# The causal convolution of a float32 block: VectorE's taps added in place in the PSUM bank, fewer taps on TensorE and GpSimd, weight splits of the stage on GpSimd

## The chip, the core and the metric

One core of one Trainium2 chip runs the whole program in one launch. The metric is device time in microseconds (us); lower is better. The kernel before took 2717.13 us (median of three runs, 2713.91 to 2719.76).

## What is computed

A block with a residual stream x of 512 tokens by 1024 features, in float32: two attention layers, four feed-forward modules, a state-space module and a convolution module. The change lies in the convolution module alone:

```python
def conv_mixer(h, w_in, b_in, dw, dw_b, ln_g, ln_b, w_out, b_out):
    z = h @ w_in + b_in
    a, g = jnp.split(z, 2, axis=-1)
    z = a * jax.nn.sigmoid(g)
    z = lax.conv_general_dilated(z, dw[:, None, :].astype(z.dtype), window_strides=(1,),
                                 padding=[(CONV_W - 1, 0)],
                                 dimension_numbers=('NWC', 'WIO', 'NWC'),
                                 feature_group_count=D_MODEL) + dw_b
    z = jax.nn.silu(layernorm(z, ln_g, ln_b))
    return z @ w_out + b_out
```

CONV_W is 31 and each of the 1024 features has its own 31 weights: y[t] is the sum over 31 taps of dw[tap] * z[t - 30 + tap]. One tap over a tile of 128 features by 512 tokens is a multiplication by one number per feature and an addition.

## The kernel before

Features stand on the 128 partitions, so the 1024 features of the convolution are eight tiles, f0 to f7, of 128 x 512. Matrices are multiplied at float32 accuracy in three passes of float32r matmuls (`mm3`, lines 159 to 161): every operand is kept as a high part and a low part, and high x high, high x low and low x high are added up in PSUM. Weights are streamed from DRAM by `load` (line 134): a DMA on SP's queue, a copy to the high part on ScalarE (line 148), and the low part as the difference on VectorE, or on GpSimd for the tile numbers in `self.on_pool` and for the first four tiles of a stage (line 153). In this stage `on_pool` is empty. A tile is 128 x 1024, and a feature tile of the input projection takes two.

`conv` (line 1165) is a software pipeline over the eight feature tiles, with three steps.

- `enter(f)`: the input projection (48 matmuls of 512 columns; f0 and f1 go together, in halves of 256 columns), the sigmoid on ScalarE (line 1208), z = a * sigmoid on VectorE (line 1211, out of PSUM, into a tile of 542 columns with 30 zeros ahead). Then the accumulator b: its first tap on ScalarE (line 1214), and further taps in which ScalarE makes the product (line 1184) and GpSimd adds it (line 1185). Then z is split in two parts for TensorE (lines 1218, 1219).
- `taps(f)`, one turn later: the first NTAP[f] taps on TensorE. GpSimd writes diagonal matrices of the weights (line 1230), and three matmuls of 512 columns for each tap add up in a PSUM bank `pc` (two banks take turns, `pjav`). The taps that are left go to VectorE, each one SCALAR_TENSOR_TENSOR in place on b (line 1187).
- `leave(f)`, three turns after `enter`: y = b + pc in another order of tokens (VectorE, line 1242), and a matmul with ones that gathers the mean (line 1244).

The 31 taps of a tile are shared out by two tables, which give 76 taps to TensorE, 52 to ScalarE with GpSimd (8 of them ScalarE's first ones, so 44 additions on line 1185), and 120 to VectorE:

```python
CLAG = 1, 3
NTAP, PTAP = (6, 6, 7, 8, 10, 10, 14, 15), (6, 8, 8, 8, 8, 8, 4, 2)
```

Behind the loop come the variance (lines 1256 to 1267), the normalisation with SiLU (lines 1272, 1273) and the output projection. A scheduler sets each engine's order of instructions when the program is built, so work of neighbouring feature tiles is interleaved on every engine, and engines then run their queue in order, held by semaphores.

Of the kernel before, what the change touches and what calls it, by code (L numbers as in the profile page):

```python
# [14 lines left out]
P = 128  # L15
# [50 lines left out]
class Kern:  # L66
# [30 lines left out]
    # how many tiles of a kind are alive at most; kinds of one size share a count  # L97
# [83 lines left out]
    def pow_(self, r, n):  # L181
        """r ^ -0.5 in place"""
        self.nc.gpsimd.tensor_tensor(out=r, in0=r, in1=self.mh.to_broadcast([P, n]), op=ALU.pow)  # L183

    def rsq(self, ss, n, div, eps):
        """(ss / div + eps)^-0.5"""
        r = self.st(n)
        self.nc.gpsimd.tensor_scalar(out=r, in0=ss, scalar1=1.0 / div, scalar2=eps, op0=ALU.mult, op1=ALU.add)
        self.pow_(r, n)
        return r  # L190

# [1 line left out]
    def prenorm(self, xt, g, dest, t):  # L193
        """xt [128, 1024] natural; dest(k0) -> AP [128, 4, 2, 128] for k0 = 0, 4"""
# [14 lines left out]
    def to_parts(self, src, dst):  # L209
        """src [128, 512] natural -> dst [128, 4, 2, 128]: transposed, split"""  # L210
        nc = self.nc
        tp = self.ps("tp", [P, 4, P])
        for i in range(4):
            nc.tensor.transpose(tp[:, i], src[:, i * P:(i + 1) * P], self.ident)  # L214
        self.splith(dst[:, :, 0], dst[:, :, 1], tp)
# [6 lines left out]
    def chain(self, t, y0, ss0, ps1, gpost, mul, nxt, bias=None):  # L222
        """x_t += rms(y_t) * gpost * mul (y0 is already times gpost), then the next norm"""
# [18 lines left out]
    def half0(self, ps, gpost, mul, bias=None):  # L242
        """the first half of y: sum of squares and y * gpost in SBUF"""
# [17 lines left out]
    def out_proj(self, key0, key1, lhs, gpost, mul, nxt, bias=None, group=1):  # L261
        """y = lhs @ w (8 k tiles), natural, then chain; lhs(k, t) -> (h, l);
        in the first half of y the token tiles go together by groups"""
# [87 lines left out]
    def attn(self, l, nxt):  # L351
# [3 lines left out]
        # tables and small parameters of the layer  # L355
# [27 lines left out]
        def roped(ab, rq):  # L383
            # ab [128, 2 (cos, sin), groups, 2, 16] -> rq [128, groups, 2, 16]
# [20 lines left out]
        def chunk_d(ci):  # L405
# [6 lines left out]
            for t in range(T):  # L412
# [15 lines left out]
                # q: [h h l l], k: [h l h l]  # L428
# [95 lines left out]
        # gates: silu(g) = g * (1 + tanh(g / 2)) / 2, the half is in the heads' factors  # L524
# [117 lines left out]
        def unit_out(u):  # L642
            """[vh|vl]^T P^T summed over the parts and turned, then the head's norm"""
# [29 lines left out]
            # (sum + 64 eps d1^2)^-0.5; the factor 8 is in sub  # L673
# [36 lines left out]
        # projections emitted along with the units  # L710
# [15 lines left out]
        def advance(f, end):  # L726
            """a projection goes on to its next step"""
# [93 lines left out]
    def sincos(self, cos, sin, y, n):  # L821
# [23 lines left out]
        # quadrant  # L845
# [43 lines left out]
    def s5_params(self):  # L889
# [23 lines left out]
        # discretised input matrix factor  # L913
# [18 lines left out]
        # |a|^4 and the unit phasor of a^4 with its doublings  # L932
# [9 lines left out]
        # cos and sin of phi * chunk for the first 16 chunks, by doubling  # L942
# [7 lines left out]
    def double(self, dst, src, s, js, m):  # L950
        """chunks m to 2m of dst from chunks 0 to m of src"""
# [9 lines left out]
    def s5_batch(self, b):  # L961
        """the matrices of four pairs of groups, in steps"""
# [9 lines left out]
        def cprod(src, w, re, im, negative):  # L972
            """(re, im) = src * w, or its conjugate"""
# [10 lines left out]
        # the place of the input matrices is free now  # L984
# [10 lines left out]
        # state output  # L995
# [9 lines left out]
        # Toeplitz part  # L1005
# [20 lines left out]
    def s5(self, nxt):  # L1026
# [20 lines left out]
        def enter(n):  # L1047
            """the chunks of four pairs, turned, times the input matrices"""
# [29 lines left out]
        def rotate_back(n):  # L1078
# [6 lines left out]
            # the state before each chunk  # L1085
# [57 lines left out]
        # the first four together: the last features come late  # L1143
# [16 lines left out]
    HOOK = 3, 1.5  # L1160
    CLAG = 1, 3
    GRP = 2, 2
    NTAP, PTAP = (6, 6, 7, 8, 10, 10, 14, 15), (6, 8, 8, 8, 8, 8, 4, 2)

    def conv(self, nxt):
# [14 lines left out]
        def tap(out, z, f, i, pool=False):  # L1180
            w = cp[:, f, 5 + i:6 + i]
            if pool:
                prod = self.tl("tap", [P, 512])
                nc.scalar.activation(prod, z[:, i:i + 512], AF.Copy, scale=w)  # L1184
                g.tensor_tensor(out=out, in0=out, in1=prod, op=ALU.add)  # L1185
            else:
                v.scalar_tensor_tensor(out=out, in0=z[:, i:i + 512], scalar=w, in1=out, op0=ALU.mult, op1=ALU.add)  # L1187

        def project(fs):
            """the first two halves of the features go together, by halves of the tokens"""  # L1190
# [11 lines left out]
        def enter(f):  # L1202
            npe, ndv = self.NTAP[f], self.NTAP[f] + self.PTAP[f]
# [9 lines left out]
            b = self.tl("cb", [P, 512])  # L1213
            nc.scalar.activation(b, z[:, npe:npe + 512], AF.Identity, scale=cp[:, f, 5 + npe:6 + npe], bias=cp[:, f, 2:3])
            for i in range(npe + 1, ndv):
                tap(b, z, f, i, True)
            zz = self.tl("zz", [P, 2, 542], F32R)
            nc.scalar.activation(zz[:, 0], z, AF.Copy)
            g.tensor_tensor(out=zz[:, 1], in0=z, in1=zz[:, 0].bitcast(F32), op=ALU.subtract)
            F[f].update(z=z, zz=zz, b=b)  # L1220

        def taps(f):
            npe, ndv = self.NTAP[f], self.NTAP[f] + self.PTAP[f]
            z, zz, b = F[f]["z"], F[f]["zz"], F[f]["b"]
# [9 lines left out]
            for i in range(ndv, 31):  # L1234
                tap(b, z, f, i)

        def leave(f):
            """from the order of time to the order of the token tiles"""
# [6 lines left out]

        for i in range(8 + self.CLAG[1]):
            for stage, lag in ((enter, 0), (taps, self.CLAG[0]), (leave, self.CLAG[1])):
                if 0 <= i - lag < 8:
                    stage(i - lag)
        ident2 = self.ident.unsqueeze(1).to_broadcast([P, 2, P])  # L1250
        t2 = "p (t c) -> p t c"
        for hf in range(2):
# [7 lines left out]
            # the variance stands on every partition: its diagonal blocks give a column per token  # L1260
# [81 lines left out]
def _layout(np, a):  # L1342
    """the inputs, laid out for the loads"""
# [25 lines left out]
    # feature order of the state-space part: (j, g2, h), group g = j + 32 g2  # L1369
# [49 lines left out]
    def bd(v):  # L1419
        # v [64 groups, 64 states, 16] -> [(g2, p), 32, (g2, h)], zero off the diagonal blocks  # L1420
# [39 lines left out]
```

## Time and profile before

| | |
|---|---|
| median of three runs | 2717.13 us (2713.91 to 2719.76) |
| profiled execution: span from its first to its last instruction | 2716.2 us |
| TensorE busy in it | 2579.7 us (95%) |
| VectorE busy | 1522.4 us (56%) |
| ScalarE busy | 1043.4 us (38%) |
| GpSimd busy | 709.4 us (26%) |
| HBM traffic | 239.61 MB read, 20.97 MB written |

The profile gives no time of its own for the profiled execution beside its span; the span lies 0.9 us below the median of the runs and inside their range. The shares are averages over stages with different limits, so the stage of the change has to be read by itself. In the rows, PE is TensorE's matmuls, PEld its weight loads, DVE VectorE, ACT ScalarE, POOL GpSimd; `L1187` is line 1187 of the program above, and `t` stands for any tile. A row's duration and the distance from one start to the next are different things, and both are used.

### The profile page before, as it was taken

The page shows a single profiled execution, that of the slowest core. Times are in us where ns is not written, and L with a number is a line of the kernel's source. Part 1 is how long each engine was busy: PE and PEld are TensorE (multiplying, and loading weights), DVE is VectorE, ACT ScalarE, POOL GpSimd, SP SyncE. Part 2 cuts the span into 40 slices and gives each one's busy share as a digit, 9 for nine tenths or more (in the row PEclk, how much of TensorE's full clock was granted, in tenths as well). Part 3 has the DMA queues.
Part 4 walks back from the last instruction along what each step waited for, and adds up shares of the span by engine and source line. Part 5 has one row for each costly group of instructions (what it writes and reads, how often), then busy time and mean ns, then how long its engine had stood idle before and what let it go on. Part 6 is the DMA issues. An engine that isn't in the chain of part 4 may idle for free.

```text
span 2716.2 us, 34572 instructions
## 1 busy us (share of the span) xinstructions
PE 2579.7 (95%) x13512; PEld 2190.4 (81%) x13512; DVE 1522.4 (56%) x2301; ACT 1043.4 (38%) x1977; POOL 709.4 (26%) x892
## 2 busy tenths in 40 slices
PE   8998999989999999899999999999999768999998
PEld 7987899878888888888888888888888546888887
DVE  7787587885688722694533324333226997533322
ACT  5567554675334422323422223322225323422221
POOL 4652245522265500331200002000006872200000
PEclk9999999999999999899999999999999889999999
DMA  4221232112235523442222222222222001222221
GB/s 148 74 66 62 78 108 74 61 62 83 82 136 198 196 98 127 149 177 94 97 97 94 94 101 86 101 95 96 97 101 86 31 31 41 99 93 96 98 94 70
DMA packets 68899, 262.81 MB, mean 97 GB/s; under 512 B 7936, under 2 KB 8448, under 8 KB 64384
## 3 DMA queue, kind: packets, MB, share of 16 engines
q1 hardware_dynamic: 68736, 260.61, 27.4%
q8 instruction: 106, 1.74, 0.3%
q14 instruction: 57, 0.47, 0.1%
HBM read 239.61 MB, written 20.97 MB: 96 GB/s over the span
## 4 chain that ended last, share of the span: by engine, by line
PE 47%; DVE 6%; POOL 2%; issue 1%; ACT 0%; POOLq 0%; DVEq 0%; ACTq 0%
PE t L160 15%; PE t L161 15%; PE t L159 15%; DVE t L1187 4%; POOL t L1230 1%; DVE t L153 1%; POOL t L153 0%; POOL t L1185 0%; PE t L214 0%; DVE t L1242 0%; DVE t L1256 0%; DVE t L1211 0%; ACT t L200 0%; PE t L1102 0%; ACT t L232 0%
## 5 line engine op out<-in xcount | busy, mean ns | idle before, releaser
L159 PE MATMUL t<-t,t 128*128 128x512 f32 (+2 forms) x3596 | 1320.8, 369 | 39.3 <-DVE t L1242 21.8
L160 PE MATMUL t<-t,t 128*128 128x512 f32 (+2 forms) x3596 | 1321.2, 368 | 8.8 <-DVE t L167 3.6
L161 PE MATMUL t<-t,t 128*128 128x512 f32 (+2 forms) x3596 | 1318.5, 368 | 2.5 <-DVE t L167 2.4
L153 DVE TENSOR_TENSOR t<-t,t 128x1024 fp32r<-128x1024 f32 (+2 forms) x326 | 413.3, 1270 | 723.5 <-ACT t L148 488.1
L159 PEld LDWEIGHTS t<-t,t 128*128 128x128 f32 x3596 | 681.6, 190 | 159.4 <-issue 17.1
L160 PEld LDWEIGHTS t<-t,t 128*128 128x128 f32 x3596 | 683.3, 190 | 124.8 <-DVE t L167 6.4
L161 PEld LDWEIGHTS t<-t,t 128*128 128x128 f32 x3596 | 682.6, 190 | 117.2 <-DVE t L167 4.2
L148 ACT ACTIVATE t<-t 128x1024 fp32r<-128x1024 f32 (+2 forms) x370 | 384.2, 1045 | 535.1 <-PE t L160 454.7
L235 POOL TENSOR_SCALAR t<-t,t 128x1 f32<-128x1 f32 x32 | 10.7, 334 | 1327.2 <-ACT t L232 1325.9
L166 ACT ACTIVATE t<-t 128x512 fp32r<-128x512 f32 (+3 forms) x316 | 155.6, 517 | 298.0 <-DVE t L297 121.2
L167 DVE TENSOR_TENSOR t<-t,t 128x512 fp32r<-128x512 f32 (+3 forms) x316 | 199.1, 647 | 81.9 <-ACT t L166 81.7
L153 POOL TENSOR_TENSOR t<-t,t 128x512 fp32r<-128x512 f32 (+4 forms) x90 | 162.2, 1820 | 66.2 <-ACT t L148 52.4
L296 ACT ACTIVATE t<-t 128x512 f32<-128x512 f32 x88 | 52.6, 598 | 301.5 <-PE t L161 295.7
L1187 DVE SCALAR_TENSOR_TENSOR t<-t,t,t 128x512 f32<-128x512 f32 x120 | 143.4, 1240 | 3.7 <-POOL t L1185 2.7
L555 ACT ACTIVATE t<-t,t 128x512 f32<-128x512 f32 (+1 forms) x176 | 113.5, 654 | 39.6 <-DVE t L553 37.2
L553 DVE TENSOR_REDUCE t<-t 128x1 f32<-128x512 f32 (+1 forms) x160 | 105.6, 681 | 16.2 <-PE t L571 7.5
L297 DVE TENSOR_TENSOR t<-t,t 128x512 f32<-128x512 f32 x88 | 60.5, 687 | 83.0 <-PE t L161 82.7
L621 DVE TENSOR_TENSOR t<-t,t 128x512 fp32r<-128x512 f32 x112 | 76.1, 685 | 36.1 <-ACT t L616 29.7
L1185 POOL TENSOR_TENSOR t<-t,t 128x512 f32<-128x512 f32 x44 | 78.5, 1786 | 25.3 <-ACT t L1184 23.2
L958 POOL TENSOR_TENSOR t<-t,t 128x64 f32<-128x64 f32 (+3 forms) x112 | 65.8, 606 | 66.3 <-DVE t L886 48.3
L183 POOL TENSOR_TENSOR t<-t,t 128x1 f32<-128x1 f32 (+2 forms) x98 | 74.0, 756 | 6.9
L976 DVE TENSOR_TENSOR t<-t,t 128x256 f32<-128x256 f32 x128 | 65.3, 574 | 17.7 <-DMA t<-in_s5bc 17.4
(220 smaller groups left out, 2228.8 us busy)
## 6 DMA issues: line engine op xcount, KB each, us to landing
t<-in_W SPq DMA_DIRECT2D x356, 512.0 KB, 3.5
mats<-t SPq DMA_DIRECT2D x16, 1024.0 KB, 4.3
t<-mats SPq DMA_DIRECT2D x16, 1024.0 KB, 6.1
t<-in_gv SPq DMA_DIRECT2D x19, 512.0 KB, 4.1
t<-in_W SPq DMA_DIRECT2D x24, 384.0 KB, 3.2
t<-in_W SPq DMA_DIRECT2D x8, 480.0 KB, 4.1
t<-in_x SPq DMA_DIRECT2D x4, 512.0 KB, 7.1
t<-in_mem SPq DMA_DIRECT2D x4, 512.0 KB, 6.3
```

What stands on the lines that cost most here:

```text
L148: nc.scalar.activation(h[:, :c], raw[:, :c], AF.Copy)
L153: eng.tensor_tensor(out=l[:, o:o + m], in0=raw[:, o:o + m], in1=h[:, o:o + m].bitcast(F32), op=ALU.subtract)
L159: mm(out, lhs[0], rhs[0], start=start, stop=False)
L160: mm(out, lhs[0], rhs[1], start=False, stop=False)
L161: mm(out, lhs[1], rhs[0], start=False, stop=stop)
L166: nc.scalar.activation(h, src, AF.Copy)
L167: nc.vector.tensor_tensor(out=l, in0=src, in1=h.bitcast(F32), op=ALU.subtract)
L553: v.tensor_reduce(out=mx[:, q * w:q * w + w], in_=part, axis=AX.X, op=ALU.max, negate=True)
L555: act.activation(e[:, i], part[:, i - q * w], AF.Exp, bias=mx[:, i:i + 1], accum_out=u["d"][:, i:i + 1])
L621: v.tensor_tensor(out=lo, in0=tp, in1=h.bitcast(F32), op=ALU.subtract)
L1185: g.tensor_tensor(out=out, in0=out, in1=prod, op=ALU.add)
L1187: v.scalar_tensor_tensor(out=out, in0=z[:, i:i + 512], scalar=w, in1=out, op0=ALU.mult, op1=ALU.add)
```

## The change

The diff, without lines that only lose a comment:

```diff
-    CLAG = 1, 3
+    CLAG = 1, 1, 2
+    CPOOL = tuple(range(12))
     GRP = 2, 2
-    NTAP, PTAP = (6, 6, 7, 8, 10, 10, 14, 15), (6, 8, 8, 8, 8, 8, 4, 2)
+    NTAP, PTAP = (6, 6, 6, 6, 6, 6, 7, 8), (4, 5, 5, 5, 5, 5, 4, 3)
...
         def enter(f):
...
-            b = self.tl("cb", [P, 512])
-            nc.scalar.activation(b, z[:, npe:npe + 512], AF.Identity, scale=cp[:, f, 5 + npe:6 + npe], bias=cp[:, f, 2:3])
-            for i in range(npe + 1, ndv):
-                tap(b, z, f, i, True)
             zz = self.tl("zz", [P, 2, 542], F32R)
             nc.scalar.activation(zz[:, 0], z, AF.Copy)
             g.tensor_tensor(out=zz[:, 1], in0=z, in1=zz[:, 0].bitcast(F32), op=ALU.subtract)
+            b = self.tl("cb", [P, 512])
+            nc.scalar.activation(b, z[:, npe:npe + 512], AF.Identity, scale=cp[:, f, 5 + npe:6 + npe], bias=cp[:, f, 2:3])
+            for i in range(npe + 1, npe + npl):
+                prod = self.tl("tap", [P, 512])
+                nc.scalar.activation(prod, z[:, i:i + 512], AF.Copy, scale=cp[:, f, 5 + i:6 + i])
+                g.tensor_tensor(out=b, in0=b, in1=prod, op=ALU.add)
...
         def taps(f):
...
-            for i in range(ndv, 31):
-                tap(b, z, f, i)
+
+        def more(f):
+
+            z, pc = F[f]["z"], F[f]["pc"]
+            for i in range(self.NTAP[f] + self.PTAP[f], 31):
+                v.scalar_tensor_tensor(out=pc, in0=z[:, i:i + 512], scalar=cp[:, f, 5 + i:6 + i], in1=pc, op0=ALU.mult, op1=ALU.add)
...
-        for i in range(8 + self.CLAG[1]):
-            for stage, lag in ((enter, 0), (taps, self.CLAG[0]), (leave, self.CLAG[1])):
+        self.on_pool = self.CPOOL
+        for i in range(8 + self.CLAG[2]):
+            for stage, lag in ((enter, 0), (taps, self.CLAG[0]), (more, self.CLAG[1]), (leave, self.CLAG[2])):
                 if 0 <= i - lag < 8:
                     stage(i - lag)
+        self.on_pool = ()
```

By the new tables TensorE has 51 taps (25 fewer, 75 matmuls fewer), ScalarE and GpSimd 36 (28 additions on GpSimd instead of 44), and VectorE 161 instead of 120. VectorE's taps no longer add onto the SBUF tile b but onto the PSUM bank in which TensorE has just added up its own; they come behind the matmuls of their tile. All twelve weight tiles of f2 to f7 have their low part made on GpSimd instead of VectorE (the four of f0 and f1 were there already, in halves). `leave` comes two turns after `enter` instead of three. The z tile is split for TensorE ahead of GpSimd's taps.

Three places in the built programs. The first is VectorE's queue where the z of a late feature tile is made. In the kernel before, at f6 (L1187 is a tap, its first name the tile it adds onto; L1211 z; L1242 `leave`):

```order
L1211 SCALAR_TENSOR_TENSOR t3205_19016<-t3202_18964,t2_64,t3204_19014 128x4x128 [waits Activation_49]
L1187 SCALAR_TENSOR_TENSOR t3162_18735<-t3161_18732,t2_64,t3162_18735 128x512 [waits DVE_49]
L1187 SCALAR_TENSOR_TENSOR t3140_18598<-t3139_18595,t2_64,t3140_18598 128x512 [waits DVE_49]
L1187 SCALAR_TENSOR_TENSOR t3183_18873<-t3182_18870,t2_64,t3183_18873 128x512 [waits Pool_49]
L1187 SCALAR_TENSOR_TENSOR t3162_18735<-t3161_18732,t2_64,t3162_18735 128x512 [waits DVE_49]
L1242 TENSOR_TENSOR t3195_18949<-t3140_18598,t3171_18761 128x512 [waits DVE_49]
L1187 SCALAR_TENSOR_TENSOR t3183_18873<-t3182_18870,t2_64,t3183_18873 128x512 [waits DVE_49]
L1187 SCALAR_TENSOR_TENSOR t3162_18735<-t3161_18732,t2_64,t3162_18735 128x512 [waits DVE_49]
L1187 SCALAR_TENSOR_TENSOR t3183_18873<-t3182_18870,t2_64,t3183_18873 128x512 [waits DVE_49]
L1187 SCALAR_TENSOR_TENSOR t3162_18735<-t3161_18732,t2_64,t3162_18735 128x512 [waits DVE_49]
```

and in the changed one, at f7 (L1235 is a tap, L1204 z):

```order
L1235 SCALAR_TENSOR_TENSOR t3176_18856<-t3150_18707,t2_64,t3176_18856 128x512 [waits DVE_49]
L1235 SCALAR_TENSOR_TENSOR t3193_18981<-t3169_18836,t2_64,t3193_18981 128x512 [waits DVE_49]
L1242 TENSOR_TENSOR t3195_19023<-t3152_18713,t3176_18856 128x512 [waits DVE_49]
L1204 SCALAR_TENSOR_TENSOR t3205_19090<-t3202_19038,t2_64,t3204_19088 128x4x128 [waits Activation_49]
L1235 SCALAR_TENSOR_TENSOR t3193_18981<-t3169_18836,t2_64,t3193_18981 128x512 [waits DVE_49] x11
L1235 SCALAR_TENSOR_TENSOR t3210_19104<-t3187_18964,t2_64,t3210_19104 128x512 [waits PE_49,Pool_49]
L1235 SCALAR_TENSOR_TENSOR t3193_18981<-t3169_18836,t2_64,t3193_18981 128x512 [waits DVE_49]
L1235 SCALAR_TENSOR_TENSOR t3210_19104<-t3187_18964,t2_64,t3210_19104 128x512 [waits DVE_49]
L1235 SCALAR_TENSOR_TENSOR t3193_18981<-t3169_18836,t2_64,t3193_18981 128x512 [waits DVE_49]
```

Before, taps of two or three feature tiles alternate, each on an SBUF tile. Now they are on PSUM banks (t3176, t3193 and t3210 are the banks of f4, f5 and f6), the first tap of a bank waits for TensorE, and between stretches that alternate stand runs on one bank, such as the eleven of f5. In the whole queue the tap in front is on the same bank for 90 of the 161 taps; before, it was on the same tile for 28 of 120.

The second place is GpSimd's queue at the start of the loop. Before (L1185 is an addition of a product, L1219 the low part of z, L1230 diagonal matrices):

```order
L1185 TENSOR_TENSOR t3089_18307<-t3089_18307,t3090_18309 128x512 [waits Activation_49]
L1185 TENSOR_TENSOR t3089_18307<-t3089_18307,t3091_18312 128x512 [waits Activation_49,Pool_49]
L1185 TENSOR_TENSOR t3089_18307<-t3089_18307,t3092_18315 128x512 [waits Activation_49,Pool_49]
L1219 TENSOR_TENSOR t3095_18324<-t3088_18304,t3095_18324 128x542 [waits DVE_49,Activation_49]
L1185 TENSOR_TENSOR t3089_18307<-t3089_18307,t3093_18318 128x512 [waits Pool_49]
L1230 TENSOR_TENSOR t3108_18359<-t2_64,t1_63 128x768
L1230 TENSOR_TENSOR t3108_18359<-t2_64 128x768
L1185 TENSOR_TENSOR t3089_18307<-t3089_18307,t3094_18321 128x512 [waits Pool_49]
L1185 TENSOR_TENSOR t3098_18332<-t3098_18332,t3099_18334 128x512 [waits Activation_49]
L1219 TENSOR_TENSOR t3106_18355<-t3097_18329,t3106_18355 128x542 [waits DVE_49,Activation_49]
L1185 TENSOR_TENSOR t3098_18332<-t3098_18332,t3100_18337 128x512 [waits Pool_49]
L1185 TENSOR_TENSOR t3098_18332<-t3098_18332,t3101_18340 128x512 [waits Activation_49,Pool_49]
```

and in the changed program (L1214, L1208 and L1226 are the same three things, L153 a weight split):

```order
L153 TENSOR_TENSOR t3106_18389<-t3104_18386,t3105_18388 128x1024 [waits DMAHW0_49,PE_49,Activation_49]
L153 TENSOR_TENSOR t3109_18395<-t3107_18392,t3108_18394 128x1024 [waits DMAHW2_49,PE_49,Activation_49]
L1208 TENSOR_TENSOR t3089_18307<-t3088_18304,t3089_18307 128x542 [waits Activation_49]
L1214 TENSOR_TENSOR t3090_18310<-t3090_18310,t3091_18312 128x512 [waits Activation_49]
L1214 TENSOR_TENSOR t3090_18310<-t3090_18310,t3092_18315 128x512 [waits Activation_49,Pool_49]
L153 TENSOR_TENSOR t3125_18518<-t3123_18515,t3124_18517 128x1024 [waits DMAHW3_49,PE_49,Activation_49]
L1214 TENSOR_TENSOR t3090_18310<-t3090_18310,t3093_18318 128x512 [waits Pool_49]
L1226 TENSOR_TENSOR t3103_18344<-t2_64,t1_63 128x768
L1226 TENSOR_TENSOR t3103_18344<-t2_64 128x768
L153 TENSOR_TENSOR t3128_18524<-t3126_18521,t3127_18523 128x1024 [waits DMAHW4_49,PE_49,Activation_49]
L1208 TENSOR_TENSOR t3096_18326<-t3095_18323,t3096_18326 128x542 [waits Activation_49]
L1214 TENSOR_TENSOR t3097_18329<-t3097_18329,t3098_18331 128x512 [waits Activation_49]
```

The low part of f0's z is now ahead of the additions, and four weight splits of 128 x 1024 have come in between (eight more follow).

The third place is TensorE's queue near the end of the loop in the changed program, where the matmul with ones for f4 (L1244) stands ahead of the taps of f6, which go into the same bank as f4's:

```order
L159 MATMUL t3193_18981<-t3170_18839,t3194_18982 128x512
L160 MATMUL t3193_18981<-t3170_18839,t3194_18982 128x512
L161 MATMUL t3193_18981<-t3170_18839,t3194_18982 128x512
L1244 MATMUL t3070_18077<-t3195_19023,t2_64 128x512 [waits DVE_49]
L159 MATMUL t3210_19104<-t3188_18967,t3211_19105 128x512 [waits Activation_49,Pool_49]
L160 MATMUL t3210_19104<-t3188_18967,t3211_19105 128x512
L161 MATMUL t3210_19104<-t3188_18967,t3211_19105 128x512 [waits Pool_49]
L159 MATMUL t3210_19104<-t3188_18967,t3211_19105 128x512
```

Both wait until VectorE has finished all of f4's taps and its `leave`; TensorE runs its queue in order.

## Rows read from the trace of the kernel before

**Rows 1.** The page: busy tenths of the span in 40 slices of 67.9 us.

```profile
PE   8998999989999999899999999999999768999998
DVE  7787587885688722694533324333226997533322
```

**Rows 2.** Stretches: us, PE, PEld, DVE, ACT, POOL busy (instructions), PE clock, DMA share, GB/s.

```profile
2079.00:2277.00 198.00, 144.20 (x572) 110.38 (x570) 182.48 (x155) 56.42 (x83) 144.25 (x80) 0.87 0.13 46
2125.00:2141.00 16.00, 1.30 (x4) 0.53 (x3) 16.00 (x16) 2.68 (x5) 7.63 (x7) 0.63 0.19 66
1900.00:1980.00 80.00, 80.00 (x348) 65.13 (x347) 21.02 (x20) 18.21 (x20) 0.00 (x0) 1.00 0.29 99
```

**Rows 3.** Chain of waits, 2050 to 2300 us: shares by line; start, us, what.

```profile
by line: DVE t L1187 44.6%; issue 7.0%; PE t L160 6.8%; PE t L161 6.6%; PE t L159 6.6%; POOL t L1230 5.9%; DVE t L153 5.3%; POOL t L1185 3.6%; DVE t L1242 2.8%; DVE t L1256 2.2%; DVE t L1211 2.1%; POOL t L1219 1.4%; DVE t L1272 1.1%; PE t L
...
2095.66 1.79 DVE t L1187
...
2273.72 1.06 DVE t L1242
2274.83 1.14 PE t L1244 x2
```

**Rows 4.** Groups, 2079 to 2277 us: count | busy us, mean ns | idle before, releasers.

```profile
L1187 DVE SCALAR_TENSOR_TENSOR t<-t,t,t 128x512 f32<-128x512 f32 x120 | 143.4, 1240 | 3.7 <-POOL t L1185 2.7
L1185 POOL TENSOR_TENSOR t<-t,t 128x512 f32<-128x512 f32 x44 | 78.5, 1786 | 25.3 <-ACT t L1184 23.2
L153 DVE TENSOR_TENSOR t<-t,t 128x1024 fp32r<-128x1024 f32 x15 | 25.8, 1723 | 10.6 <-ACT t L148 9.1 <-PE t L160 1.5
L1211 DVE SCALAR_TENSOR_TENSOR t<-t,t,t 128x512 f32<-128x512 f32 x8 | 9.0, 1130 | 0.0
L1242 DVE TENSOR_TENSOR t<-t,t 128x512 f32<-128x512 f32 x8 | 8.5, 1062 | 1.6 <-PE t L161 1.6
```

**Rows 5.** VectorE in order of time: start us, us from first start to last end.

```profile
2262.16 10.20 DVE L1187 SCALAR_TENSOR_TENSOR t<-t,t,t 128x512 f32<-128x512 f32 x13
...
2186.10 6.04 DVE L1187 SCALAR_TENSOR_TENSOR t<-t,t,t 128x512 f32<-128x512 f32 x9
...
2166.07 11.94 DVE L1187 SCALAR_TENSOR_TENSOR t<-t,t,t 128x512 f32<-128x512 f32 x7
...
2161.41 1.12 DVE L1211 SCALAR_TENSOR_TENSOR t<-t,t,t 128x512 f32<-128x512 f32 x1
2162.38 1.41 DVE L1187 SCALAR_TENSOR_TENSOR t<-t,t,t 128x512 f32<-128x512 f32 x1
```

**Rows 6.** GpSimd in order of time, the same columns.

```profile
2090.48 1.47 POOL L1230 TENSOR_TENSOR t<-t,t 128x768 fp32r<-128x768 f32 x1
...
2160.90 2.34 POOL L1230 TENSOR_TENSOR t<-t 128x1024 fp32r<-128x1024 f32 x1
...
2167.32 10.14 POOL L1185 TENSOR_TENSOR t<-t,t 128x512 f32<-128x512 f32 x6
...
2259.04 1.26 POOL L1185 TENSOR_TENSOR t<-t,t 128x512 f32<-128x512 f32 x1
2260.26 1.32 POOL L1219 TENSOR_TENSOR t<-t,t 128x542 fp32r<-128x542 f32 x1
```

**Rows 7.** Groups of the whole span, shapes apart: weight splits on GpSimd.

```profile
L153 POOL TENSOR_TENSOR t<-t,t 128x1024 fp32r<-128x1024 f32 x18 | 44.9, 2502 | 10.4 <-ACT t L148 9.2 <-PE t L161 1.1
```

**Rows 8.** Groups, 1700 to 2055 us (last: 1930 to 2330): L167 reads PSUM, L153 not.

```profile
L153 DVE TENSOR_TENSOR t<-t,t 128x1024 fp32r<-128x1024 f32 x62 | 75.9, 1224 | 199.7 <-ACT t L148 130.5 <-issue 65.8 <-PE t L160 3.3
L167 DVE TENSOR_TENSOR t<-t,t 128x512 fp32r<-128x512 f32 x24 | 16.3, 684 | 0.0
...
L167 DVE TENSOR_TENSOR t<-t,t 128x256 fp32r<-128x256 f32 x16 | 6.1, 420 | 1.6 <-ACT t L166 1.6
```

**Rows 9.** VectorE, then ScalarE, in order of time (L1256 reads PSUM and SBUF).

```profile
2275.99 5.39 DVE L1256 SCALAR_TENSOR_TENSOR t<-t,t 128x256 f32<-128x256 f32 x16 [1.22 <-PE t L1244]
...
2078.08 0.69 ACT L1208 ACTIVATE t<-t,t 128x512 f32<-128x512 f32 x1 [0.39 <-PE t L161]
```

More of the change, by code (lines that the diff above doesn't have):

```diff
@@ L1178, in conv @@
         cs = []
[L1180 to L1187, printed above, removed]
         def project(fs):
@@ L1202, in enter @@
         def enter(f):
-            npe, ndv = self.NTAP[f], self.NTAP[f] + self.PTAP[f]
+            npe, npl = self.NTAP[f], self.PTAP[f]
             if f != 1:
@@ L1219, in enter @@
             g.tensor_tensor(out=zz[:, 1], in0=z, in1=zz[:, 0].bitcast(F32), op=ALU.subtract)
+            b = self.tl("cb", [P, 512])
[4 more added lines that the diff above has]
+                g.tensor_tensor(out=b, in0=b, in1=prod, op=ALU.add)
             F[f].update(z=z, zz=zz, b=b)
         def taps(f):
-            npe, ndv = self.NTAP[f], self.NTAP[f] + self.PTAP[f]
-            z, zz, b = F[f]["z"], F[f]["zz"], F[f]["b"]
+            npe = self.NTAP[f]
+            zz = F[f]["zz"]
             F[f]["pc"] = pc = self.pjav()
```

## The prediction

> **What bounds the kernel now.** The page comes first. Over the whole span TensorE is the busy engine, but in its slices [rows 1] there is one dip, slices 32 to 35, in which PE falls to 6 and 7 tenths while DVE stands at 9. That is the convolution, so the page's average is of no use here. The stretches come next [rows 2]: from the first z to the last mean (2079 to 2277 us, 198 us) VectorE is busy 182.5 us, GpSimd 144.3 and TensorE 144.2, and for 16 us from 2125 TensorE does next to nothing. In the chain of waits [rows 3] VectorE's taps, line 1187, hold 44.6% of 2050 to 2300 us, and the last link ahead of the variance is `leave` at 2273.72 and the matmul for the mean, which ends at 2275.97. So this stage ends when VectorE has done its taps, and a change is worth here what it takes off VectorE's queue.
>
> The groups tell what those taps cost [rows 4]: 120 take 143.4 us, 1.24 us each. The rows in order of time [rows 5] show three prices. Nine that alternate between tiles, with GpSimd held up all the while, take 6.04 us, 0.67 each. Thirteen on one tile, with GpSimd at rest, take 10.20 us, 0.785 each: a tap that waits for the tap just ahead of it pays 0.115 us more. And seven that run against GpSimd take 11.94 us, 1.71 each, while the six GpSimd additions of that stretch take 10.14, 1.69 each, where one alone takes 1.26 [rows 6]: addition and tap run one for one, and a pair of them needs 1.7 us. Both have two inputs in SBUF. Line 1211, which reads one input from PSUM, starts at 2161.41 in the middle of a GpSimd instruction of 2.34 us and still takes 1.12 us, its usual duration [rows 4 to 6]. An instruction with one input in PSUM does not take part in this.
>
> **What the change does to VectorE.** The 120 taps and their 143.4 us go, and so do ten of the twelve weight splits, 10 x 1.72 = 17 us [rows 4] (the other two lie ahead of 2079). There come 161 taps whose inputs are one of SBUF and one of PSUM. By the row of line 1211 they are free of GpSimd. No instruction before writes to PSUM from VectorE, so the price of one has to be bounded. From below: line 1256 reads PSUM and takes 5.39 / 16 = 0.34 us for 256 elements [rows 9], and 256 elements more cost 0.684 - 0.420 = 0.26 (line 167 in two sizes, [rows 8]), hence 0.60, or 0.715 behind its own predecessor. From above: line 1211, also out of PSUM and with a scalar per feature, lets the next instruction start 0.97 us after itself [rows 5], 0.30 more than an SBUF tap, but its strided order is a likely cause. I take the SBUF prices, 0.67 and 0.785, because they are for the same instruction with the same scalar, and because reading PSUM shows no surcharge: at 0.264 us per 256 elements line 167 takes 0.16 us over the streaming of its 512 elements out of PSUM, and line 153 takes 1.224 us for 1024 out of SBUF, 0.17 over it [rows 8]. By the orders above, 90 of the 161 follow a tap on their own bank: 90 x 0.785 + 71 x 0.67 = 118.2 us.
>
> [...]
>
> **When the first tap can start.** It now waits for TensorE's taps of f0. In TensorE's new order these stand behind the rest of f1's projection (46 matmuls of 256 columns), all 48 of f2 and nine of f3. From 2078.1 us, when TensorE has released f0's sigmoid [rows 9], that is 46 x 0.115 + (48 + 9 + 18) x 0.23 = 22.5 us, at 80 us / 348 = 0.23 us for 512 columns [rows 2] and half of it for 256; the end of the last matmul adds some 0.4. So the first tap starts near 2101, against 2095.66 before, and VectorE mostly rests until then. GpSimd is not later: behind f0's z it has the low part, two additions, a split of 2.50, an addition and two diagonal matrices of 1.47 [rows 6, 7], about 11 us from 2081.
>
> **The sum.** From 2101: taps 118.2; five z at 0.97 = 4.9; eight `leave` at 1.0 (the 1.06 of [rows 4] less the overlap with the next) = 8; four splits for the output projection, which stay on VectorE and still have two SBUF inputs, at 1.72 = 6.9; waits for TensorE at the change of banks, some five of 1 us = 5. Together 143 us, to 2244; the mean behind the last `leave` adds 1.2 [rows 3], 2245.2. Before it was 2276.0. The stage loses 30.8 us, and what follows is unchanged. The profiled execution's span of 2716.2 becomes 2685.4; it lies 0.9 us below the median of the runs shown (2717.13), so I forecast 2686.3, rounded **2686 us**.
>
> **What the other edits cost.** TensorE loses 75 matmuls of 0.23, 17 us, worth nothing by itself: from 2101 it has 366 matmuls of 0.23 and eight means of some 1.2 us left, 94 us beside VectorE's 143, which hides them. If VectorE's time fell under 94, TensorE would be next. GpSimd's part from 2079 on is ten splits of 2.50, sixteen rows of diagonal matrices (27 us), eight low parts of 1.32 and 28 additions of 1.26 [rows 6, 7], 98 us without VectorE in its way; the 165 us from first z to last mean cover it too. The splits now stand in GpSimd's queue among additions that wait for ScalarE, so a late product would delay the next weights; ScalarE loses 16 products and has room, busy 56 of 198 us [rows 2]. Splitting z first and `leave` a turn earlier cost nothing beside VectorE's queue, and SP's DMAs are the same in number and order.
>
> **Rivals.** (1) **TensorE's taps come too late** for VectorE near the end. The taps of f6 go into f4's bank and stand behind f4's mean, so TensorE rests until `leave`; then VectorE has about ten taps on the other bank, 7.9 us, in which TensorE must do the mean (1.14) and 18 matmuls (4.1). At full clock the 5.2 us fit. After pauses the granted clock fell before: 0.63 on the mean over the 16 us of rest [rows 2]. [...] Against it: the pauses are shorter, about 8 us. (2) **The tap in PSUM is dear**, the one that ends on the other side: reading and writing one bank in the same instruction, which no row shows, could cost as line 1211 does, 0.30 us more on each of 161, 48 us: 2734, slower. It decides from 30.8 / 161 = 0.19 us a tap on. A mild surcharge, up to 0.10 us a tap, is counted within the forecast. For it speaks only that nothing here was measured; against it the PSUM reads without surcharge [rows 8]. (3) **The contention stays**, because one SBUF input is enough for it: some fifty GpSimd instructions from 2101 on would each cost VectorE 1.7 - 0.7 = 1.0 us: 2736. Line 1211's undisturbed 1.12 us speaks against it. (4) The gain is given back in the following stages, or the taps do not move: the built order shows all 161 on banks, and nothing behind the mean changes, so I give this little.
>
> **How the numbers follow.** Forecast 0.73, rival 1 0.12, rival 2 0.09, rival 3 0.04, no difference 0.02. The forecast's own range: at the lower price (71 x 0.60 + 90 x 0.715 = 107), without waits (5) and with splits at 1.22 each [rows 8] (2) 18 us less, 2668; with a third of line 1211's surcharge, 0.10 us a tap, 16 more, 2702. For 8 in 10 the range runs from 2671 to 2707: it takes in rival 1 and leaves out most of rivals 2 and 3. About 0.2%, 5.4 us, is what a measurement of this kernel can tell from no change. Faster by more than that: 0.85, from the forecast and rival 1; within it 0.02; slower 0.13, from rivals 2 and 3.
>
> **What would show it.** In the profile after, 161 taps on line 1235, 0.67 or 0.785 us from one to the next, the same beside GpSimd as without it; GpSimd's additions near 1.26 instead of 1.79; the first tap near 22 us behind the first z and the last mean 165 us behind it (before 196.8); VectorE with almost no pauses in between. Taps 0.95 us apart mean rival 2; one that is long only beside GpSimd, rival 3; VectorE idle ahead of the first tap of a bank, with TensorE named, rival 1. The forecast is wrong if the stage shortens as said and the whole does not.

## The result, and the profile after

The changed kernel takes 2684.53 us (median of four runs, 2680.91 to 2690.54), beside 2717.61 us for the kernel before on the same chip (four runs, 2713.91 to 2719.76). The ratio is 0.9884, with a 95% interval of 0.9868 to 0.9899: some 32 us faster. 2686 us were forecast, in a range of 2671 to 2707. The profiled execution took 2685.91 us, with a span of 2684.1.

In the stage's slices of the page, PE stays under 9 tenths in two (33 and 34), where in [rows 1] it did in three (32 to 34; the prediction's "32 to 35" is one too many). The other digits under 9 lie outside the stage:

```profile
PE   7998999989999999989999999999999966999998
DVE  7788577875589832595533323433324697533322
```

The first z starts at 2076.58 us and the last mean ends at 2242.2, so the stage takes 165.6 us where it took 196.8; what follows it takes 441.9 (before 440.2). The stretches, with the columns of [rows 2]; the first is the stage from first z to last mean:

```profile
2076.00:2243.00 167.00, 124.20 (x502) 94.68 (x500) 137.13 (x184) 47.16 (x68) 97.96 (x68) 0.86 0.16 57
...
2099.00:2151.00 52.00, 52.00 (x222) 41.47 (x221) 47.40 (x64) 17.12 (x24) 46.94 (x35) 1.00 0.21 72
2151.00:2203.00 52.00, 36.05 (x131) 26.42 (x129) 49.78 (x67) 14.99 (x21) 28.43 (x21) 0.84 0.11 41
2203.00:2243.00 40.00, 13.16 (x30) 7.18 (x30) 36.25 (x52) 0.34 (x2) 0.00 (x0) 0.61 0.07 26
```

VectorE is busy 137.1 of 167 us, and from its first tap on it hardly rests: 133.4 of 144 us in the last three rows. GpSimd fell from 144.3 us to 98.0. Which prices did this is in the groups of the stage, first VectorE's, then GpSimd's; they answer to [rows 4]:

```profile
L1235 DVE SCALAR_TENSOR_TENSOR t<-t,t,t 128x512 f32<-128x512 f32 x161 | 116.3, 752 | 10.9 <-PE t L161 7.5
L1204 DVE SCALAR_TENSOR_TENSOR t<-t,t,t 128x512 f32<-128x512 f32 x8 | 9.1, 1142 | 21.0 <-ACT t L1201 21.0
L1242 DVE TENSOR_TENSOR t<-t,t 128x512 f32<-128x512 f32 x8 | 8.4, 1053 | 0.1
L153 DVE TENSOR_TENSOR t<-t,t 128x1024 fp32r<-128x1024 f32 x4 | 4.9, 1222 | 1.1 <-ACT t L148 1.1
...
L1214 POOL TENSOR_TENSOR t<-t,t 128x512 f32<-128x512 f32 x28 | 37.5, 1339 | 2.0 <-ACT t L1213 1.1
L153 POOL TENSOR_TENSOR t<-t,t 128x1024 fp32r<-128x1024 f32 x11 | 26.4, 2409 | 4.9 <-ACT t L148 4.6 <-issue 0.3
```

There are 161 taps in place of 120, and they take 116.3 us in place of 143.4: 0.752 us each against 1.240. A GpSimd addition takes 1.34 us against 1.79. VectorE in order of time, with the columns of [rows 5], shows that GpSimd no longer counts for a tap:

```profile
2098.76 13.42 DVE L1235 SCALAR_TENSOR_TENSOR t<-t,t,t 128x512 f32<-128x512 f32 x17 [3.67 <-PE t L161]
2113.40 6.02 DVE L1235 SCALAR_TENSOR_TENSOR t<-t,t,t 128x512 f32<-128x512 f32 x9 [1.22 <-PE t L161]
...
2121.29 11.83 DVE L1235 SCALAR_TENSOR_TENSOR t<-t,t,t 128x512 f32<-128x512 f32 x15
...
2187.06 7.34 DVE L1235 SCALAR_TENSOR_TENSOR t<-t,t,t 128x512 f32<-128x512 f32 x11 [0.32 <-PE t L161]
...
2219.63 7.34 DVE L1235 SCALAR_TENSOR_TENSOR t<-t,t,t 128x512 f32<-128x512 f32 x11 [0.59 <-PE t L161]
...
2227.84 11.04 DVE L1235 SCALAR_TENSOR_TENSOR t<-t,t,t 128x512 f32<-128x512 f32 x14
```

And GpSimd beside the fifteen taps from 2121.29 on:

```profile
2121.32 2.41 POOL L153 TENSOR_TENSOR t<-t,t 128x1024 fp32r<-128x1024 f32 x1 [4.59 <-ACT t L148]
2123.70 1.47 POOL L1226 TENSOR_TENSOR t<-t,t 128x768 fp32r<-128x768 f32 x1
2125.13 1.47 POOL L1226 TENSOR_TENSOR t<-t 128x768 fp32r<-128x768 f32 x1
2126.55 1.37 POOL L1208 TENSOR_TENSOR t<-t,t 128x542 fp32r<-128x542 f32 x1
2127.88 1.30 POOL L1214 TENSOR_TENSOR t<-t,t 128x512 f32<-128x512 f32 x1
2129.13 2.42 POOL L153 TENSOR_TENSOR t<-t,t 128x1024 fp32r<-128x1024 f32 x1
2131.50 4.05 POOL L1214 TENSOR_TENSOR t<-t,t 128x512 f32<-128x512 f32 x3
```

GpSimd works without a pause here, and the fifteen taps on one bank take 11.83 us, 0.79 each. The fourteen from 2227.84, with GpSimd at rest, take 11.04, 0.79 each too. Nine that alternate between banks take 6.02, 0.67 each. These are the two prices of [rows 5] for a tap on an SBUF tile without GpSimd in its way, to within 0.01 us. In the whole trace a tap follows a tap 148 times: 90 times by 0.77 to 0.80 us, 54 times by 0.65 to 0.67, and the four longer distances are the waits for TensorE. So no tap is slowed by GpSimd.

### The profile page after: what moved, and what is told of

Read it like the earlier page. It is cut to its first block, busy times and chain, and to the rows that moved or that the text cites. A ratio compares the mean times of both kernels' runs of the same rounds, so it can differ in the third digit from the quotient of the medians.

```text
span 2684.1 us, 34384 instructions
## 1 busy us (share of the span) xinstructions
PE 2558.3 (95%) x13437; PEld 2170.8 (81%) x13437; DVE 1471.3 (55%) x2330; ACT 1034.2 (39%) x1961; POOL 666.4 (25%) x880
## 4 chain that ended last, share of the span: by engine, by line
PE 51%; DVE 3%; POOL 1%; ACT 1%; issue 0%; DVEq 0%; POOLq 0%; ACTq 0%
PE t L160 17%; PE t L161 17%; PE t L159 17%; DVE t L1235 2%; POOL t L153 0%; PE t L1244 0%; PE t L214 0%; PE t L1261 0%; DVE t L1242 0%; ACT t L200 0%; ACT t L148 0%; ACT t L232 0%; PE t L1102 0%; DVE t L206 0%; PE t L1103 0%
## 5 line engine op out<-in xcount | busy, mean ns | idle before, releaser
L159 PE MATMUL t<-t,t 128*128 128x512 f32 (+3 forms) x3571 | 1309.5, 369 | 15.2 <-ACT t L166 12.3
L160 PE MATMUL t<-t,t 128*128 128x512 f32 (+3 forms) x3571 | 1308.8, 367 | 6.8 <-DVE t L167 3.3
L161 PE MATMUL t<-t,t 128*128 128x512 f32 (+3 forms) x3571 | 1304.5, 367 | 2.5 <-DVE t L167 2.4
L159 PEld LDWEIGHTS t<-t,t 128*128 128x128 f32 x3571 | 674.4, 189 | 133.8 <-ACT t L166 17.4
L153 DVE TENSOR_TENSOR t<-t,t 128x1024 fp32r<-128x1024 f32 (+2 forms) x314 | 389.8, 1244 | 706.1 <-ACT t L148 510.8
L160 PEld LDWEIGHTS t<-t,t 128*128 128x128 f32 x3571 | 675.7, 189 | 123.1 <-DVE t L167 6.0
L161 PEld LDWEIGHTS t<-t,t 128*128 128x128 f32 x3571 | 675.4, 189 | 115.1 <-DVE t L167 4.2
L167 DVE TENSOR_TENSOR t<-t,t 128x512 fp32r<-128x512 f32 (+3 forms) x316 | 198.9, 647 | 75.4 <-ACT t L166 75.2
L153 POOL TENSOR_TENSOR t<-t,t 128x512 fp32r<-128x512 f32 (+4 forms) x102 | 191.0, 1889 | 78.8 <-ACT t L148 56.8
L1235 DVE SCALAR_TENSOR_TENSOR t<-t,t,t 128x512 f32<-128x512 f32 x161 | 116.3, 752 | 10.9 <-PE t L161 7.5
L206 DVE SCALAR_TENSOR_TENSOR t<-t,t,t 128x512 f32<-128x512 f32 x72 | 57.9, 845 | 26.9 <-POOL t L183 26.9
```

Source lines behind the costliest of these rows:

```text
L153: eng.tensor_tensor(out=l[:, o:o + m], in0=raw[:, o:o + m], in1=h[:, o:o + m].bitcast(F32), op=ALU.subtract)
L159: mm(out, lhs[0], rhs[0], start=start, stop=False)
L160: mm(out, lhs[0], rhs[1], start=False, stop=False)
L161: mm(out, lhs[1], rhs[0], start=False, stop=stop)
L1235: v.scalar_tensor_tensor(out=pc, in0=z[:, i:i + 512], scalar=cp[:, f, 5 + i:6 + i], in1=pc, op0=ALU.mult, op1=ALU.add)
```

## The experiments

Each edit is against the changed kernel. "The loop" is the time from the start of the first z to the end of the last mean. All medians are of runs beside the kernel before on the same chip, 2719.27 us for the first four and 2716.10 for the last four.

| kernel | median, us | ratio to before (95%) | loop, us |
|---|---|---|---|
| taps back on the SBUF tile | 2733.56 | 1.0053 (1.0038 to 1.0068) | 208.3 |
| splits back on VectorE | 2691.91 | 0.9898 (0.9884 to 0.9913) | 168.1 |
| tables of before | 2688.63 | 0.9886 (0.9869 to 0.9902) | 166.9 |
| taps in PSUM alone | 2675.37 | 0.9839 (0.9825 to 0.9854) | 151.9 |
| the change again | 2687.28 | 0.9893 (0.9876 to 0.9911) | 165.6 |
| taps in PSUM alone, again | 2677.31 | 0.9858 (0.9841 to 0.9874) | 151.7 |
| tables between | 2672.82 | 0.9841 (0.9826 to 0.9856) | 147.5 |
| leave a step later | 2671.28 | 0.9836 (0.9820 to 0.9851) | 151.6 |

### Taps back on the SBUF tile

```diff
         def more(f):
-            z, pc = F[f]["z"], F[f]["pc"]
+            z, b = F[f]["z"], F[f]["b"]
...
-                v.scalar_tensor_tensor(out=pc, ... in1=pc, op0=ALU.mult, op1=ALU.add)
+                v.scalar_tensor_tensor(out=b, ... in1=b, op0=ALU.mult, op1=ALU.add)
```

> The changed kernel with one thing undone: VectorE's 161 taps add onto the SBUF tile b again; tables, splits on GpSimd and lags stay. Theory (the gain is the place of the taps: one input in PSUM keeps them out of GpSimd's way): 161 taps at 0.72 us, and some 60 GpSimd instructions from the first z on that each cost VectorE 1.0 us more, less the 15 us by which the first tap can start earlier: 2720 to 2740 us, taps of 1.0 us and more on the mean, GpSimd's additions back near 1.7. Rival (splits off VectorE and the lighter tables carry the gain): no more than 2695.

Measured: 2733.56 us, 0.5% slower than before, as the theory expected. The tables, the splits and the order of the steps are those of the change (the scheduler interleaves the taps of the tiles differently), and 161 taps on b cost what the contention makes of them: here a tap and a GpSimd instruction that both read two SBUF inputs hold each other up, a tap to 1.150 us and an addition to 1.648. The groups of the loop, and behind them the last fifteen taps, all on one tile, with GpSimd at rest:

```profile
L1235 DVE SCALAR_TENSOR_TENSOR t<-t,t,t 128x512 f32<-128x512 f32 x161 | 177.5, 1150 | 4.2 <-POOL t L1214 2.5
...
L1214 POOL TENSOR_TENSOR t<-t,t 128x512 f32<-128x512 f32 x28 | 46.0, 1648 | 0.6
L153 POOL TENSOR_TENSOR t<-t,t 128x1024 fp32r<-128x1024 f32 x11 | 30.2, 2749 | 3.6 <-ACT t L148 3.6
...
2274.60 11.78 DVE L1235 SCALAR_TENSOR_TENSOR t<-t,t,t 128x512 f32<-128x512 f32 x15
```

A tap takes 1.150 us in place of 0.752, and a GpSimd addition 1.648 in place of 1.339. With GpSimd at rest the taps on b have the change's price, 0.79 us each, so the difference is GpSimd's and not that of SBUF as such. The first tap even starts 12.5 us earlier, 9.7 us behind the first z in place of 22.2, because b doesn't wait for TensorE; the loop is still 42.7 us longer. So the place of the taps alone is worth about that much with these tables, and the rest of the change, without it, is a loss.

### Splits back on VectorE; tables of before; both

Three kernels keep the taps in PSUM and undo one or both of the other parts.

```diff
-    CPOOL = tuple(range(12))
+    CPOOL = ()
```

> The changed kernel with its weight splits on VectorE again (the pool set empty); taps in PSUM and tables stay. Theory: ten splits of 1.22 us return to VectorE, those of f2 and f3 into its wait ahead of the first tap, where they cost nothing, six others 7 us at most; GpSimd's diagonal matrices come earlier: 2683 to 2692. Rival (taking the splits off VectorE is a main part of the gain, 17 us): 2700 or more.

```diff
-    NTAP, PTAP = (6, 6, 6, 6, 6, 6, 7, 8), (4, 5, 5, 5, 5, 5, 4, 3)
+    NTAP, PTAP = (6, 6, 7, 8, 10, 10, 14, 15), (6, 8, 8, 8, 8, 8, 4, 2)
```

> The changed kernel with the tables of before (76 taps on TensorE, 44 additions on GpSimd, 120 taps on VectorE), taps in PSUM, splits on GpSimd. Theory: VectorE has 41 taps fewer, 30 us, but GpSimd now has splits 25, diagonal matrices 40, low parts 11 and additions 55, 131 us, and TensorE some 110, so most of VectorE's saving is lost to waits for these: 2680 to 2695. Rival (the lighter tables are what makes the stage shorter): 2700 or more.

The fourth kernel has both edits, which leaves the taps in PSUM and the new order of the steps:

> Tables of before and all splits on VectorE; only the taps are moved onto the PSUM bank (with the lags and the order of the z split of the change). Theory (the place of the taps is the gain): 120 taps at 0.73 us are 88 us in place of 143, and with ten splits of 1.22, z and leave VectorE has 115 us behind a first tap at 22 us, GpSimd 106 and TensorE 110: 2668 to 2682, better than the whole change, whose other parts then give back about 10 us. Rival (splits and tables carry it): 2700 to 2717.

Measured: 2691.91, 2688.63 and 2675.37 us, each inside the range of its theory. Each part undone alone makes no difference that the totals can show (0.9898 and 0.9886 beside 0.9884 and, measured again, 0.9893 for the change), and the loop is 2.5 and 1.3 us longer; both undone together gain some 10 us on the change. Their stretches, from first z to last mean, say why (the columns of [rows 2]). Splits on VectorE:

```profile
2083.40:2251.50 168.10, 121.20 (x494) 92.71 (x492) 147.19 (x192) 46.39 (x65) 77.60 (x57) 0.85 0.16 54
```

Tables of before, with the splits on GpSimd, and there the longest wait of the taps (engine, line, what it waited for: us, times, longest):

```profile
2080.30:2247.20 166.90, 140.90 (x553) 107.23 (x551) 112.66 (x140) 56.10 (x81) 130.75 (x92) 0.90 0.17 55
```

```profile
DVE t L1235 <- PE t L161: 39.2, 8, 12.9
```

In the first, VectorE has 161 taps and the splits, 147.2 of 168.1 us, while GpSimd is idle for more than half. In the second, GpSimd has 44 additions and the splits, 130.8 of 166.9 us, and VectorE stands for 39.2 us in front of TensorE's taps, 12.9 of it ahead of the first one, where the fourth kernel does splits; TensorE itself waits 7.6 us for GpSimd's diagonal matrices, in the other kernels of this group and in the change not at all. By their loops, new tables go better with the splits on GpSimd (165.6 against 168.1 us) and old tables with the splits on VectorE (151.9 against 166.9), and the old pair is the better of the two.

### The change and "taps in PSUM alone" on one chip

The difference between the change and its first part came from two sets of runs, so both were measured again on one chip.

> The change itself, unaltered, for a comparison on the chip of the next three. Expected by both theories: 2680 to 2691, loop from the first z to the last mean 164 to 168 us.

> The taps in PSUM alone (tables of before, all splits on VectorE), beside the change on one chip. Theory: the smaller tables and the splits on GpSimd give back time, since VectorE, on 161 taps and 137 of 167 us, is the change's bound, and with the tables of before it has 120 taps (88 us) and 127 of 153 us: 10 to 14 us under the change, 2670 to 2680. Rival: the difference of the two so far is spread of the stages outside the loop: within 4 us of the change.

Measured: 2687.28 and 2677.31 us, 10.0 apart, at the near end of what was expected; the loops are 165.6 and 151.7, 13.9 apart. The rival (within 4 us) falls. The loop of "taps in PSUM alone", its stretch and its groups:

```profile
2079.00:2230.70 151.70, 133.31 (x553) 103.46 (x552) 126.46 (x150) 56.21 (x81) 115.30 (x81) 0.94 0.19 59
```

```profile
L1235 DVE SCALAR_TENSOR_TENSOR t<-t,t,t 128x512 f32<-128x512 f32 x120 | 88.3, 754 | 12.1 <-PE t L161 9.4
L153 DVE TENSOR_TENSOR t<-t,t 128x1024 fp32r<-128x1024 f32 x14 | 23.7, 1700 | 10.7 <-ACT t L148 10.7
...
L1214 POOL TENSOR_TENSOR t<-t,t 128x512 f32<-128x512 f32 x44 | 62.8, 1429 | 4.2 <-ACT t L1213 1.7
```

VectorE has 120 taps, 88.3 us, where the change gives it 161, 116.3 us; the splits that it takes back cost 23.7 against 4.9. That leaves it 9 us less work, and TensorE is busy 133.3 of 151.7 us and waits 18.4 us for a `leave`, where in the change it sits for 42.0 us in front of one. The splits still read two SBUF inputs, and still contend: 1.70 us each, and an addition takes 1.43, where the change has 1.22 and 1.34.

### Tables between, and leave a step later

```diff
-    CPOOL = tuple(range(12))
+    CPOOL = ()
...
-    NTAP, PTAP = (6, 6, 6, 6, 6, 6, 7, 8), (4, 5, 5, 5, 5, 5, 4, 3)
+    NTAP, PTAP = (6, 6, 6, 7, 8, 10, 12, 13), (6, 8, 8, 8, 8, 8, 5, 3)
```

> Taps in PSUM, splits on VectorE, and TensorE's taps between the two tables, (6, 6, 6, 7, 8, 10, 12, 13), with GpSimd's (6, 8, 8, 8, 8, 8, 5, 3): 126 taps on VectorE in place of 120. Theory: with the tables of before, the last two tiles end on TensorE (14 and 15 taps of 4 matmuls each), so that 4 taps taken from there shorten the end: 2 to 4 us under the kernel with the tables of before. Rival: VectorE's chain still sets the end, and the 6 taps more cost 6 x 0.75 = 4.5 us: 4 to 5 us over it.

Measured: 2672.82 us, 4.5 under "taps in PSUM alone", and a loop of 147.5, 4.2 shorter: the theory's sign, a little more than its 2 to 4 us (a tap is three matmuls, not the four that it counts). The intervals of the two ratios overlap (0.9841 to 0.9874 and 0.9826 to 0.9856), so it is the loop that carries this: the same kernel gave 151.9 and 151.7 us, and the change twice 165.6. The six taps more do cost VectorE the rival's 4.5 us (92.8 against 88.3), but the splits take 3.0 less, and the waits for TensorE's taps 5.0 less (4.4 against 9.4). The end of VectorE's queue shows the place. With the tables of before, VectorE stands there twice in front of TensorE's late taps, for 4.09 and 1.13 us; with the tables between, for 0.82 and 0.50:

```profile
2204.20 10.26 DVE L1235 SCALAR_TENSOR_TENSOR t<-t,t,t 128x512 f32<-128x512 f32 x13 [4.09 <-PE t L161]
2215.59 0.75 DVE L1235 SCALAR_TENSOR_TENSOR t<-t,t,t 128x512 f32<-128x512 f32 x1 [1.13 <-PE t L161]
```

```profile
2199.05 9.46 DVE L1235 SCALAR_TENSOR_TENSOR t<-t,t,t 128x512 f32<-128x512 f32 x12 [0.82 <-PE t L161]
2209.02 3.39 DVE L1235 SCALAR_TENSOR_TENSOR t<-t,t,t 128x512 f32<-128x512 f32 x5 [0.50 <-PE t L161]
```

The last kernel keeps the tables of before and the splits on VectorE:

```diff
-    CLAG = 1, 1, 2
+    CLAG = 1, 1, 3
-    CPOOL = tuple(range(12))
+    CPOOL = ()
...
-    NTAP, PTAP = (6, 6, 6, 6, 6, 6, 7, 8), (4, 5, 5, 5, 5, 5, 4, 3)
+    NTAP, PTAP = (6, 6, 7, 8, 10, 10, 14, 15), (6, 8, 8, 8, 8, 8, 4, 2)
```

> Taps in PSUM, tables of before, splits on VectorE, and the leave of a tile one step later (lag 3 in place of 2). Theory: VectorE and TensorE stand in the loop because a leave in program order waits for the GpSimd additions and for the last tap of its own tile; a step later it finds both done: 2 to 3 us under the kernel with lag 2. Rival: the waits only move to the end, where one more leave stands behind the last tap: the same within 2 us, or 1 to 3 us over it.

Measured: a loop of 151.6 us against 151.7, as the rival says. The wait has only moved, to one of 7.04 us in front of a single tap near the end:

```profile
2216.82 0.76 DVE L1235 SCALAR_TENSOR_TENSOR t<-t,t,t 128x512 f32<-128x512 f32 x1 [7.04 <-PE t L161]
```

The median is 6.0 us lower all the same, 2671.28. The intervals of the two ratios overlap (0.9841 to 0.9874 and 0.9820 to 0.9851), the profiled spans differ by 0.5 us the other way (2673.3 and 2672.8), and the loop gives no reason. Whether this edit gains anything stays open. The best kernel whose gain its trace explains is the one with the tables between, 0.9841.

## Why the prediction was right, point by point

**The price of a tap** held. Forecast were 0.67 and 0.785 us and 118.2 us for 161; measured are 0.67 and 0.79, and 116.3 us of busy time, or 119.7 with the 3.4 us of idle time before line 1235 that is no wait for TensorE (10.9 - 7.5). The 90 distances of the higher price are the 90 that the built order had given. Writing to PSUM has no surcharge that the rows could show: in the kernel with the taps back on b, 21 taps in a row take 13.99 us, 0.67 each, the same as nine in PSUM.

What the rows do show is a price for following one's predecessor: in the changed kernel a tap on the bank of the tap before it starts 0.79 us behind it (0.77 to 0.80, 90 times), and one on another bank 0.67 (0.65 to 0.67, 54 times). The taps that alternate wait on a semaphore too, by the orders above (`[waits DVE_49]`).

**Contention** was gone from the taps, as line 1211's 1.12 us had suggested. The first experiment shows that this is what the change lives on: with one input out of PSUM a tap takes 0.752 us, and with both in SBUF 1.150, beside the same work of GpSimd.

**The first tap** came 22.2 us behind the first z (forecast 22), and VectorE did 3.7 us of work in that stretch. The first experiment prices this wait: on b the taps start 12.5 us sooner.

**The small terms.** Waits behind the first tap: four for TensorE, 1.22, 1.74, 0.32 and 0.59 us, and 1.1 us for ScalarE, together 5.0 (forecast 5). The eight `leave` took 8.4 (forecast 8). The four splits on VectorE took 4.9 us, not 6.9: I had taken the contended mean of [rows 4], and they ran at 1.22, the price of [rows 8]. Two of them met a GpSimd addition, and it was the additions that paid, with 2.19 and 1.71 us. The last mean took longer than the 1.2 us of the forecast, since VectorE waited 2.17 us for it:

```profile
2242.20 1.08 DVE L1258 SCALAR_TENSOR_TENSOR t<-t,t 128x256 f32<-128x256 f32 x3 [2.17 <-PE t L1244]
```

The one was 2 us too dear, the other 1 us too cheap. From first tap to last mean the sum was 144 us (2101 to 2245.2); it measures 143.4 (2098.76 to 2242.2). The loop is 165.6 us, within 1 us of the forecast, and the whole 1.5 us under it. That the whole comes so close is in part luck: the first z comes 2.6 us earlier than before (2076.58 against 2079.16), and what follows the loop takes 1.7 us more, neither of which was forecast. Measured again, the same kernel starts its first z at 2078.15 and takes 2687.28 us.

**GpSimd** needed 98.0 us in the stage, as summed (98), by errors that cancel: additions a little dearer (1.34, not 1.26), eleven splits in the stretch instead of ten but a little cheaper (2.41, not 2.50), and the sixteen rows of diagonal matrices 24.8 us, not 27.

**TensorE** was called hidden, and over the whole loop it is: VectorE waits for its taps only 7.5 us, 3.7 of it ahead of the first tap. But the cover is thinner than "94 us beside 143" sounds. From 2099 to 2151 us TensorE is busy 52.00 of 52 us, with VectorE at 47.4, and the chain of waits runs through TensorE up to 2167 and for the most part through VectorE's taps only then. So "this stage ends when VectorE has done its taps" holds for the kernel before and for the second half of this one; in the first half TensorE is as much the limit. From 2099 to 2243 us it is busy 101 us where 94 were summed. The chain's shares by line, 2076 to 2243 us:

```profile
by line: DVE t L1235 26.4%; PE t L160 20.4%; PE t L159 20.3%; PE t L161 20.2%; PE t L1244 5.3%; DVE t L1242 3.0%; issue 1.3%; DVE t L1204 1.2%; DVE t L153 0.7%; ACT t L148 0.6%; DVE t L1258 0.3%; ACT t L1260 0.3%; DVEq L1235 0.0%; DVEq L153
```

**Rival 1** held in its premise and not in its effect. TensorE waits for `leave` (42.0 us in five waits), the granted clock falls (to 0.50 on the mean over the last 16 us), and VectorE hardly notices (0.9 us). The waits, then the end of the loop in stretches:

```profile
PE t L1244 <- DVE t L1242: 42.0, 5, 10.0
...
DVE t L1235 <- PE t L161: 7.5, 5, 3.7
```

```profile
2211.00:2220.00 9.00, 8.52 (x26) 5.70 (x25) 8.05 (x12) 0.00 (x0) 0.00 (x0) 0.76 0.23 89
2220.00:2226.00 6.00, 0.00 (x0) 0.00 (x0) 6.00 (x10) 0.00 (x0) 0.00 (x0) 0.68 0.00 0
2226.00:2242.00 16.00, 3.98 (x4) 1.00 (x4) 13.47 (x18) 0.00 (x0) 0.00 (x0) 0.50 0.00 0
```

The granted clock is 0.76 in the stretch in which f7's taps are made, and 0.50 only in the last 16 us. Eleven taps on the other bank take 8.66 us meanwhile, and 0.59 us of waiting is left over; with the 0.32 at the bank before, TensorE's late taps cost VectorE 0.9 us near the end. No run shows the cost for which the forecast's range made room on this rival's account; the 0.9 us are what the runs showed in its place. With fewer taps on VectorE and more on TensorE, in "taps in PSUM alone", such a wait near the end is 4.09 us.

**Rivals 2 and 3** fell with the price of a tap. What rival 3 forecast, 2736 us, is close to what the kernel has with the contention put back, 2733.56.

What the prediction did not ask is whether all parts of the change help. They don't: the taps in PSUM alone, with the new order of the steps, shorten the loop from 196.8 to 151.7 us, and the smaller tables with the splits on GpSimd give 13.9 us of it back. What the new order of the steps is worth by itself was not tried, but for the `leave`, whose lag made no difference to the loop.

## What to carry to other kernels

Where VectorE and GpSimd run side by side and slow each other, an accumulator in PSUM freed both here: a tap took 0.752 us in place of 1.150 and a GpSimd addition 1.34 in place of 1.65, the tap kept the price that it has alone (0.67 or 0.79), and the result of TensorE was already there to be added to. The price was a later start, since the accumulator has to wait for TensorE: 22.2 us behind the first z in place of 9.7. And when a price falls, put it in first, alone, and share the work out anew from that profile: here VectorE's taps still ended the stage, and handing it 41 taps more cost more (28.0 us) than the splits it gave away (18.8).

## What the runs showed beside this

Which of the two engines loses, when both read two SBUF inputs, was not the same throughout one run. In the kernel with the taps back on b, VectorE in order of time, at five places:

```profile
2091.02 19.79 DVE L1235 SCALAR_TENSOR_TENSOR t<-t,t,t 128x512 f32<-128x512 f32 x11 [2.49 <-POOL t L1214]
...
2161.23 4.04 DVE L1235 SCALAR_TENSOR_TENSOR t<-t,t,t 128x512 f32<-128x512 f32 x6
...
2217.96 9.45 DVE L1235 SCALAR_TENSOR_TENSOR t<-t,t,t 128x512 f32<-128x512 f32 x8
...
2231.42 13.99 DVE L1235 SCALAR_TENSOR_TENSOR t<-t,t,t 128x512 f32<-128x512 f32 x21
...
2247.28 20.84 DVE L1235 SCALAR_TENSOR_TENSOR t<-t,t,t 128x512 f32<-128x512 f32 x20
```

And the GpSimd instructions that come in during the second, third and fourth of these, and the one at the start of the fifth:

```profile
2162.21 4.25 POOL L1208 TENSOR_TENSOR t<-t,t 128x542 fp32r<-128x542 f32 x1 [6.38 <-ACT t L1207]
...
2218.94 1.59 POOL L1208 TENSOR_TENSOR t<-t,t 128x542 fp32r<-128x542 f32 x1 [6.19 <-ACT t L1207]
...
2239.06 7.90 POOL L1226 TENSOR_TENSOR t<-t,t 128x896 fp32r<-128x896 f32 x1 [13.46 <-PE t L161]
2246.92 1.68 POOL L1226 TENSOR_TENSOR t<-t 128x896 fp32r<-128x896 f32 x1
```

In the first and the fifth stretch GpSimd is at work when they begin, and tap and GpSimd instruction take turns, one for one: the first eight taps of the first, all on one tile, start 2.18 us apart on the mean, and the first six of the fifth, where two tiles take turns, 1.91. As soon as GpSimd has nothing to do, the taps run at 0.79 and 0.66 us, so the means of these stretches (1.80 and 1.04) mix two prices. In the fourth, three tiles take turns; there the taps keep their 0.67 us, and it is GpSimd that stands: an instruction of 1.69 us in the change takes 7.90, and ends 1.6 us behind the last of these taps (2246.96 against 2245.41). The number of tiles doesn't decide this: in the second stretch two tiles take turns, and GpSimd stands as well (4.25 us for an instruction of 1.36 in the change); in the third it is three tiles, and GpSimd gets in at once, with the four taps that follow starting 1.67 to 1.74 us apart. Nor is it that VectorE was there first, since it was so in the second, third and fourth alike. What decides it is open.

The other thing is the price of following one's predecessor: 0.12 us a tap, in PSUM as in SBUF (0.79 against 0.67 in both). For the 90 taps that do, that is an estimated 11 us of VectorE's queue (90 x 0.12); an order in which they alternate was not tried.
